# One pool of 2 KB slots, accumulators opened by ScalarE, and chunk products taken ahead of their norm, in a one-core encoder layer

## The chip, the core and the metric

The kernel runs on one core of a Trainium2 chip. TensorE (PE) does the matmuls, VectorE (DVE) and ScalarE (ACT) the elementwise work, SyncE (SP) issues nearly all DMAs. The metric is the device time of one execution in microseconds; the median of the runs shown counts.

## The reference, cut to what matters

One encoder layer over two token groups, a prompt of 1024 and a sample of 256 rows, width 1024, in float32:

```python
h = x + 0.5 * swiglu(rmsnorm(x, g1), w_gate1, w_up1, w_down1)      # d_ff = 2816
proj = rmsnorm(h, gm) @ w_in                                        # 22 units of 128 columns
a = rmsnorm(banded_sink_attention(rot(aq), rot(ak), av), ga)        # window 128, 8 heads, 2 kv heads
r = silu(rg) * normalise(retention_fwd + retention_bwd)             # 4 heads of 128, chunks of 128
h = h + concat([a, r]) @ w_out
h = h + 0.5 * swiglu(rmsnorm(h, g2), w_gate2, w_up2, w_down2)
y = rmsnorm(h, g_final)
# swiglu(x, wg, wu, wd) = (silu(x @ wg) * (x @ wu)) @ wd ;  rmsnorm(x) = x * rsqrt(mean(x^2)) * g
```

## The kernel before, in words

Everything is kept transposed: 1024 features on 8 tiles of 128 partitions (KT = 8), and the 1280 tokens along the free dimension in three chunks, c = 0 and c = 1 of 512 tokens (the prompt) and c = 2 of 256 (the sample). Each operand of a large matmul is split into a rounded high part and a low part (`split`: ACT casts "hi", DVE subtracts to get "lo"), and each product is three matmuls: hi·hi, hi·lo, lo·hi (`part`, line 452).

**The two feed-forward blocks** (`ffn`, line 564) have 22 blocks of 128 hidden columns, taken in pairs t and t+11, so 11 pairs. For each pair gate (m = 0) and up (m = 1) are computed, then the activations are split, stored to DRAM (`keep`) and read back later by the down projection. Pair 0 is computed directly (`direct`): for each of gate and up the chunks 2, 0, 1 in turn, two units each. Pairs 1 to 10 use a 7/8 scheme (`product`, `seven`, `combos`): the two 512-token chunks and the two halves of the width form 2x2 blocks, and seven products of sums and differences replace eight; chunk 2 is computed plainly beside them in the banks d1 and d2. Weights come as 128x256 tiles (`fetch(..., 256)`, 8 for each product), and the sums of weights are formed by DVE on 128x256 tiles. In the first block the first chunk computed (2) runs on x·g with the row factors of the norm multiplied in behind the product (`rows2`); chunks 0 and 1 are normed first (`first`, `second`, `normed`).

The down projection (`down`, line 686) runs over groups of pairs ([0], [1, 2], [3, 4], [5, 6], [7, 8]) and adds each PSUM result into the residual h by a DVE instruction (`add`). h, 24 tiles, is loaded by `h = load()` (line 733) before the first group; each group reads nine activation products for each pair back from DRAM (`act`). `down_last` does pairs 9 and 10 and closes with the next norm.

**The middle** projects the 22 units for each chunk (`project`), runs attention blocks and retention heads in between, and the output projection (`out_unit`).

**Memory.** Work tiles live in two rings of slots: class s2, 77 slots of 128x512 (2 KB a partition), and class s1, 66 slots of 128x256 (1 KB) (`NS2, NS1`, line 394). `big(W)` picks the class by width. PSUM has 8 banks.

**Order.** All operations are recorded in program order by `Weaver` and then ordered by a list scheduler (`order`, line 219): each engine takes, of the operations that are ready, the one recorded first; DMAs may run at most 300 operations ahead of the oldest matmul not yet placed; a slot must be free, and `may` keeps the order of slots safe. Durations come from a table (`cost`, line 141); a DMA issue is counted there as 0.05 us and 2.2 us to land. The result is a fixed order for each engine; at run time each instruction waits in its queue for its semaphores. All instructions are emitted from line 372, so the profile's rows are told apart by tile names: raw = a fetched weight, whi/wlo = its parts, xh/xl = parts of an activation or factor, xa = an activation read back, h = residual, pa/pb/pc = PSUM banks.

Of the kernel before, what the change touches and what calls it, by code (L numbers as in the profile page):

```python
# [12 lines left out]
P = 128  # L13
# [78 lines left out]
class Op:  # L92
    __slots__ = ("eng", "calls", "cost", "lat", "bufs", "deps", "idx", "wait", "succ", "ready", "allocs", "kind", "at")
# [6 lines left out]
class Weaver:  # L100
# [5 lines left out]
    AHEAD = 300  # L106
    ENG = {"tensor": "PE", "vector": "DVE", "scalar": "ACT", "gpsimd": "POOL", "sync": "SP"}
# [33 lines left out]
    def cost(eng, method, a, k, outs, ins):  # L141
        n = outs[0].box[3] - outs[0].box[2] if outs else 0
        if eng == "tensor":
            if method == "transpose":
                return 0.107
            r = ins[0].buf.args[2] == F32R
            if r:
                return n / 2400 + 0.0136

            side = outs[0].box[1] - outs[0].box[0] <= 64  # L150
            return max((2.2 if side else 4) * n / 2400, 0.11 if n == 1 else 0.213)
        m = max([n] + [v.box[3] - v.box[2] for v in ins])
        ps = any(v.buf.psum for v in ins)
        if eng == "scalar":
            if a[2:3] == (AF.Identity,):
                return 0.3
            return (0.05 if ps else 0.09) + m * 0.00084 + (0.19 if "accum_out" in k else 0)
# [4 lines left out]
        if method == "tensor_scalar":  # L162
            return 0.06 + n * 0.00104 + 0.06 * (len(ins) - 1)
        if method == "tensor_tensor_reduce":
# [7 lines left out]
    def record(self, calls):  # L172
# [3 lines left out]
        for eng, method, a, k in calls:  # L176
# [15 lines left out]
            for views, wr in ((ins, False), (outs, True)):  # L192
                for v in views:
# [15 lines left out]
                    if id(b) not in op.bufs:  # L209
                        op.bufs[id(b)] = b  # L210
                        b.left += 1
                        if b.order is None and b.tag is not None:
# [3 lines left out]
                            op.allocs.append(b)  # L216
        self.ops.append(op)

    def order(self):
        import heapq  # L220

        ops = self.ops

# [64 lines left out]
        while len(out) < len(ops):  # L288
            best = None
            for e in engs:  # L290
                lim = free[e] + SLACK
                while later[e] and later[e][0][0] <= lim:
                    heapq.heappush(now[e], heapq.heappop(later[e])[1])
                held = []
                pick = None
                while now[e]:
                    i = heapq.heappop(now[e])
                    if may(ops[i]):
                        pick = (max(free[e], ops[i].ready), i)
                        heapq.heappush(now[e], i)  # L300
                        break
                    held.append(i)
# [18 lines left out]
            if i in now[e]:  # L321
                now[e].remove(i)
# [62 lines left out]
def tile_encoder_layer(ctx: ExitStack, tc: tile.TileContext, xT, wf1, w_in, w_out, wf2,  # L385
# [8 lines left out]
    NS2, NS1 = 77, 66  # L394
# [11 lines left out]
    def s2(dt=F32, name="t"):  # L406
        return nc.tile(hp, [P, 512], dt, "s2", nm(name), NS2)

# [35 lines left out]
    def halves(t, W=512):  # L444
        hi, lo = big(W, F32R, "whi"), big(W, F32R, "wlo")
# [48 lines left out]
    def norm_split(h, gcol, W):  # L494
        pb = rms_rows(h, W)
        xh, xl = [], []
        for kt, x in enumerate(h):
# [3 lines left out]
            a = big(W, F32R, "xh")  # L501
            b = big(W, F32R, "xl")
# [5 lines left out]
    def normed(h, gcol, W):  # L508
        pb = rms_rows(h, W)
# [7 lines left out]

    def pair(t, W):
        a, b = big(W, F32R, "xh"), big(W, F32R, "xl")
# [13 lines left out]
    def seven(r11, r12, r21, r22):  # L533

        def tile1(name):
            return big(256, name=name)

        yield 1, halves(r11, 256)
        yield 2, halves(r12, 256)
        s1, s2_ = tile1("s1"), tile1("s2")  # L540
        nc.vector.tensor_tensor(s1, r21, r22, op=ALU.add)
        nc.vector.tensor_tensor(s2_, s1, r11, op=ALU.add)
        yield 6, halves(s2_, 256)
        s3 = tile1("s3")
        nc.vector.tensor_tensor(s3, r11, r21, op=ALU.add)
        yield 7, halves(s3, 256)
        yield 5, halves(s1, 256)
        yield 4, halves(r22, 256)
        yield 21, halves(r21, 256)
        s4 = tile1("s4")  # L550
        nc.vector.tensor_tensor(s4, s2_, r12, op=ALU.add)
        yield 3, halves(s4, 256)
# [11 lines left out]
    def ffn(tag, wsrc, xn, xp, x2, load, after, rows2=None):  # L564
# [4 lines left out]
        keep = {}  # L569

        def product(t, m):
# [6 lines left out]
            def both(ps, ws, x, W, start, stop):  # L578
                for k, w in enumerate(ws):
                    part(ps, w, x[2 * k:2 * k + 2], W, start and k == 0, stop and k == 1)  # L580

            for (i, w0), (_, w1) in zip(*(seven(*q) for q in r)):
                w = w0, w1
                if i == 1:
                    both(X, w, xs[1], 512, True, True)
                    both(d1, w, x2[:4], 256, True, False)
                    o11 = s2(name="o11")
                    nc.scalar.copy(o11, X)
                elif i == 2:
                    both(Z, w, xs[2], 512, True, True)  # L590
# [645 lines left out]
```

## Time and profile before

| | us |
|---|---|
| median of 3 runs | 2381.1 (2379.52 to 2383.1) |
| the profiled execution | 2384.64 |
| its span, first to last instruction | 2382.7 |
| PE busy in it | 2300.1 (97%) |
| DVE busy | 1664.0 (70%) |
| ACT busy | 1011.8 (42%) |

The span falls into the first feed-forward block (up to about 900 us), the middle (to about 1540 us) and the second block. The profile's views used here are: the page, the busy time of each engine in chosen stretches, the groups of instructions, the chain of work that ended last, the waits of one engine for another, and the instructions in order of time. All refer to this one execution.

### The profile page before, as it was taken

To read this page: it belongs to the slowest core of one execution; us is meant where nothing else is said; L and a number is where in the kernel's file an instruction comes from. 1 tells how busy PE (TensorE), PEld (TensorE's weight loads), DVE (VectorE), ACT (ScalarE), POOL (GpSimd) and SP (SyncE) were. 2 spreads that over 40 slices of the span, in tenths; PEclk is the share of its full clock that TensorE was granted. 3 is DMA by queue.
4 is the path that set the end of the run, shared out by engine and by line. 5 is a ranking of instruction groups with operands and counts; after the bars stand their busy time and mean duration, and the time that the engine had idled before them with its cause. 6 is when DMAs were issued, how large, how long until landed. Compare 5 with 4: busy or idle time off the path is not lost.

```text
span 2382.7 us, 35970 instructions
## 1 busy us (share of the span) xinstructions
PE 2300.1 (97%) x12354; PEld 1948.1 (82%) x12354; DVE 1664.0 (70%) x3639; ACT 1011.8 (42%) x2297; POOL 28.2 (1%) x31
## 2 busy tenths in 40 slices
PE   7999999999799999999999999999999999989998
PEld 6888888888688888886777878888888888868887
DVE  8677766675777866655677767956776766677866
ACT  6444444443222235235667555534444444322311
POOL 0000000000000000000000000000000000000000
PEclk8999999999899999999999999999999999999999
DMA  4233343338865443230115254223443335876622
GB/s 161 95 123 123 132 147 116 111 114 290 281 197 191 142 154 107 70 106 32 32 43 180 85 168 144 66 100 126 140 153 111 114 122 188 278 250 202 191 81 89
DMA packets 230296, 330.77 MB, mean 139 GB/s; under 512 B 25824, under 2 KB 113760, under 8 KB 230112
## 3 DMA queue, kind: packets, MB, share of 16 engines
q1 hardware_dynamic: 230112, 328.47, 41.2%
q8 instruction: 97, 1.59, 0.3%
q14 instruction: 87, 0.71, 0.1%
HBM read 226.65 MB, written 101.71 MB: 138 GB/s over the span
## 4 chain that ended last, share of the span: by engine, by line
PE 88%; DVE 3%; DMA 3%; ACT 3%; issue 1%; SPq 1%; POOL 0%; POOLq 0%; DVEq 0%; ACTq 0%
PE pa L372 61%; PE pb L372 26%; ACT prob L372 2%; DMA raw<-wf 1%; SPq L372 1%; DVE prob L372 1%; DVE xn L372 1%; DVE wlo L372 1%; ACT whi L372 0%; DVE o L372 0%; DMA xa<-a_7l 0%; PE pc L372 0%; DVE xl L372 0%; ACT pt L372 0%; DVE h L372 0%
## 5 line engine op out<-in xcount | busy, mean ns | idle before, releaser
L372 PE MATMUL pa<-xh,whi 128*128 128x512 f32 (+1 forms) x2576 | 921.6, 358 | 10.3 <-ACT whi L372 3.8
L372 PE MATMUL pa<-xh,wlo 128*128 128x512 f32 (+1 forms) x2576 | 911.8, 354 | 6.1 <-DVE wlo L372 6.0
L372 PE MATMUL pa<-xl,whi 128*128 128x512 f32 (+1 forms) x2576 | 912.1, 354 | 5.6 <-DVE xl L372 5.6
L372 PEld LDWEIGHTS pa<-xh,whi 128*128 128x128 f32 x2576 | 491.5, 191 | 86.7 <-ACT whi L372 8.6
L372 PEld LDWEIGHTS pa<-xh,wlo 128*128 128x128 f32 x2576 | 490.2, 190 | 78.9 <-DVE wlo L372 12.4
L372 PEld LDWEIGHTS pa<-xl,whi 128*128 128x128 f32 x2576 | 491.3, 191 | 69.4 <-DVE xl L372 6.5
L372 PE MATMUL pb<-xa,whi 128*128 128x512 f32 (+1 forms) x1968 | 526.3, 356 | 21.3 <-DVE h L372 18.6
L372 ACT CAST whi<-raw 128x256 fp32r<-128x256 f32 (+1 forms) x676 | 304.3, 473 | 444.1 <-PE pa L372 216.0
L372 PEld LDWEIGHTS pb<-xa,whi 128*128 128x128 f32 x1968 | 349.8, 191 | 77.2 <-DVE h L372 21.9
L372 DVE TENSOR_TENSOR wlo<-raw,whi 128x256 fp32r<-128x256 f32 (+1 forms) x676 | 327.6, 505 | 107.7 <-PE pa L372 53.3
L372 ACT CAST whi<-s 128x256 fp32r<-128x256 f32 x464 | 184.2, 406 | 412.6 <-DVE s L372 211.9
L372 PE MATMUL pb<-xa,wlo 128*128 128x512 f32 (+1 forms) x984 | 348.7, 354 | 3.2 <-DVE wlo L372 3.2
L372 DVE SCALAR_TENSOR_TENSOR h<-pb,h 128x512 f32<-128x512 f32 (+1 forms) x408 | 245.9, 623 | 61.8 <-PE pb L372 59.4
L372 DVE TENSOR_TENSOR wlo<-s,whi 128x256 fp32r<-128x256 f32 x464 | 191.5, 423 | 104.6 <-PE pa L372 53.2
L372 PEld LDWEIGHTS pb<-xa,wlo 128*128 128x128 f32 x984 | 187.5, 191 | 30.9 <-DVE wlo L372 4.4
L372 DVE TENSOR_TENSOR s<-raw,raw 128x256 f32<-128x256 f32 x232 | 97.9, 422 | 86.2 <-PE pa L372 78.7
L372 DVE TENSOR_TENSOR s<-s,raw 128x256 f32<-128x256 f32 x232 | 97.1, 423 | 52.0 <-PE pa L372 34.7
L372 DVE TENSOR_TENSOR o<-o,pa 128x512 f32<-128x512 f32 x120 | 82.2, 685 | 68.9 <-PE pa L372 36.4
L372 ACT ACTIVATE sq<-h 128x512 f32<-128x512 f32 (+1 forms) x96 | 50.4, 555 | 117.1 <-DVE h L372 101.1
L372 ACT CAST xh<-s 128x512 fp32r<-128x512 f32 (+1 forms) x114 | 60.3, 537 | 81.2 <-DVE s L372 56.9
L372 DVE TENSOR_TENSOR xl<-s,xh 128x512 fp32r<-128x512 f32 (+1 forms) x114 | 65.1, 585 | 19.5 <-ACT xh L372 12.7
L372 DVE TENSOR_TENSOR sq<-sq,sq 128x512 f32<-128x512 f32 (+1 forms) x93 | 55.7, 600 | 17.1 <-ACT sq L372 12.8
(126 smaller groups left out, 1644.0 us busy)
## 6 DMA issues: line engine op xcount, KB each, us to landing
raw<-wf SPq DMA_DIRECT2D x464, 128.0 KB, 2.5
raw<-w_in SPq DMA_DIRECT2D x132, 256.0 KB, 3.1
raw<-w_out SPq DMA_DIRECT2D x48, 256.0 KB, 3.1
raw<-wf SPq DMA_DIRECT2D x32, 256.0 KB, 3.6
h<-xT SPq DMA_DIRECT2D x32, 256.0 KB, 5.4
a_1h<-xh SPq DMA_DIRECT2D x22, 256.0 KB, 2.0
a_2h<-xh SPq DMA_DIRECT2D x22, 256.0 KB, 2.1
a_1l<-xl SPq DMA_DIRECT2D x22, 256.0 KB, 2.3
```

The source lines that it names most:

```text
L372: i = getattr(getattr(self.nc, eng), method)(*[r(x) for x in a], **{m: r(x) for m, x in k.items()})
```

## The change

- **Slots.** `NS2, NS1` become 104 and 12 (before 77 and 66; the same bytes). A split tile of at most 256 columns puts hi and lo beside each other in one 2 KB slot (`two`), also when it goes to DRAM and back (one DMA of 256 KB for what were two of 128 KB).
- **Weights.** `product` fetches 128x512 tiles (4 for each product), and `seven` works on width 512 there. `down` fetches its 256-column pieces in pairs with one DMA.
- **Residual.** `down` no longer loads h ahead: the first `add` to each of the 24 tiles is an ACT copy from PSUM with the scale in it. The residual of chunk 0, 1, 2 is loaded and added by DVE behind groups 1, 2, 3.
- **First reads of the down projection.** In the up product of the last pair, behind its second of eight pieces, the nine products of pair 0 are read back (`early`).
- **Pair 0.** `direct` now goes chunk by chunk with gate and up together. In the first block chunks 2 and 0 both run on x·g ahead of their norm; the row factors are multiplied in at gate and up. Chunk 1 is normed first, chunk 0 is normed afterwards for the later pairs. A chunk-2 product uses two PSUM banks for its four results.
- **Planner.** A DMA issue is counted as 0.47 us and 2.0 us to land; some other costs are corrected. The list scheduler runs four times; from each plan a due time of every operation is worked out, which gives DVE, ACT, POOL and SP a new priority for the next plan, and the plan with the shortest span by its own table is used.

```diff
-    NS2, NS1 = 77, 66
+    NS2, NS1 = 104, 12
+    def two(W, name):
+        if W <= 256:
+            t = s2(F32R, name)
+            return t[:, :W], t[:, 256:256 + W]
+        return s2(F32R, name + "h"), s2(F32R, name + "l")
...
-                op.cost, op.lat, op.kind = 0.05, 2.2, nb
+                op.cost, op.lat, op.kind = 0.47, 2.0, nb
...
     def order(self):
+        best, prio = None, list(range(len(self.ops)))
+        for _ in range(self.PASSES):
+            out = self.arrange(prio)
+            if best is None or self.span < best[0]:
+                best = self.span, out
+            due = self.due()
...
+                if op.eng == "PE" or due[op.idx] is None:
+                    prio.append(op.idx)
+                else:
+                    j = bisect.bisect(times, (due[op.idx], 1 << 60)) - 1
+                    prio.append(min(op.idx, times[max(j, 0)][1]))
...
-            r = [[fetch(wsrc[u, :, m, i * 512 + k * 256:i * 512 + k * 256 + 256], 256)
-                  for u in (t, t + HALF) for i in range(2)] for k in range(2)]
+            r = [fetch(wsrc[u, :, m, i * 512:i * 512 + 512]) for u in (t, t + HALF) for i in range(2)]
...
+    def raw_pair(x, kt, W):
+        g = par[:, G_F1 + kt:G_F1 + kt + 1]
+        a, b = two(W, "x")
+        nc.scalar.activation(a[:, :W], x[:, :W], AF.Copy, scale=g)
+        nc.vector.scalar_tensor_tensor(b[:, :W], x[:, :W], g, a[:, :W].bitcast(F32), op0=ALU.mult, op1=ALU.subtract)
+        return a, b
...
+        def up(s, x, W, rows):
+            nc.vector.tensor_tensor(s[:, :W], s[:, :W], x[:, :W], op=ALU.mult)
+            if rows is not None:
+                nc.vector.tensor_tensor(s[:, :W], s[:, :W], rows[:, :W], op=ALU.mult)
...
+            products(2)
+            products(0)
+            close(2)
+            lead.ready(1)
+            close(0)
+            products(1)
+            lead.ready(0)
+            close(1)
...
             def add(c, d, ps, sign):
                 W = CH[c][1]
-                nc.vector.scalar_tensor_tensor(h[c][d][:, :W], ps[:, :W], 0.5 * sign, h[c][d][:, :W],
-                                               op0=ALU.mult, op1=ALU.add)
+                if h[c][d] is None:
+                    h[c][d] = big(W, name="h")
+                    nc.scalar.activation(h[c][d][:, :W], ps[:, :W], AF.Copy, scale=0.5 * sign)
+                else:
+                    nc.vector.scalar_tensor_tensor(h[c][d][:, :W], ps[:, :W], 0.5 * sign, h[c][d][:, :W],
+                                                   op0=ALU.mult, op1=ALU.add)
...
+        def early(i):
+            if i == 2:
+                first.update({j: [act(0, j)] for j in (1, 2, 6, 7, 5, 4, 3, 8, 9)})
...
-        h = load()
-        for g in ([0], [1, 2], [3, 4], [5, 6], [7, 8]):
-            down(g, h)
+        groups = [[0], [1, 2], [3, 4], [5, 6], [7, 8]]
+        for n, g in enumerate(groups):
+            down(g, h, first if n == 0 else None)
+            if 1 <= n <= 3:
+                c = n - 1
+                W = CH[c][1]
+                for d in range(KT):
+                    t = load(c, d)
+                    nc.vector.tensor_tensor(h[c][d][:, :W], h[c][d][:, :W], t[:, :W], op=ALU.add)
```

## Rows read from the trace of the kernel before

**Rows 1.** The page: engine, busy us (share of the span), instructions.
```profile
PE 2300.1 (97%) x12354; PEld 1948.1 (82%) x12354; DVE 1664.0 (70%) x3639; ACT 1011.8 (42%) x2297; POOL 28.2 (1%) x31
```

**Rows 2.** Busy us (instructions) by stretch: PE, PEld, DVE, ACT, POOL; clock, DMA share, GB/s.
```profile
0.00:120.00 120.00, 105.03 (x531) 90.85 (x532) 89.93 (x172) 67.77 (x138) 3.93 (x7) 0.91 0.38 127
120.00:540.00 420.00, 415.99 (x2175) 351.89 (x2175) 289.21 (x639) 194.18 (x438) 0.00 (x0) 1.00 0.37 125
540.00:700.00 160.00, 145.31 (x732) 122.20 (x731) 110.36 (x247) 43.52 (x107) 0.00 (x0) 0.94 0.76 259
...
1100.00:1240.00 140.00, 127.86 (x796) 92.94 (x795) 91.57 (x277) 92.21 (x238) 4.31 (x4) 0.94 0.09 31
1240.00:1440.00 200.00, 190.02 (x1285) 162.42 (x1285) 147.48 (x405) 118.53 (x286) 9.70 (x10) 0.98 0.45 146
1560.00:2040.00 480.00, 480.00 (x2536) 414.25 (x2535) 319.18 (x671) 212.01 (x487) 0.00 (x0) 1.00 0.41 136
2040.00:2120.00 80.00, 69.41 (x349) 58.01 (x348) 54.42 (x120) 22.58 (x58) 0.00 (x0) 0.94 0.89 314
```

**Rows 3.** Groups by shape, PE, 1560 to 2040 us: busy us, mean ns, idle before.
```profile
L372 PE MATMUL pa<-xh,whi 128*128 128x512 f32 x545 | 213.1, 391 | 0.0
...
L372 PE MATMUL pa<-xh,whi 128*128 128x256 f32 x301 | 84.8, 282 | 0.0
```

**Rows 4.** The chain that ended last, projections of chunk 2: start us, us, what.
```profile
1312.01 16.19 PE pa L372 x135
```

**Rows 5.** Groups by shape, PE, 120 to 540 us.
```profile
L372 PE MATMUL pa<-xh,whi 128*128 128x512 f32 x460 | 182.3, 396 | 3.9 <-DVE o L372 3.4 <-ACT whi L372 0.5
...
L372 PE MATMUL pa<-xl,whi 128*128 128x256 f32 x265 | 75.0, 283 | 0.0
```

**Rows 6.** The chain that ended last, 0 to 60 us.
```profile
5.43 4.13 DMA raw<-wf
...
10.26 8.80 PE pa L372 x48
...
27.03 5.36 DVE xn L372 x8
```

**Rows 7.** DVE instructions in order of time, 48 to 60 us: start, us.
```profile
54.60 4.90 DVE L372 TENSOR_TENSOR xl<-xn,xh 128x512 fp32r<-128x512 f32 x8
```

**Rows 8.** DMA issues on SP's queue in order of time, 0 to 112 us.
```profile
1.17 3.74 SPq L372 DMA_DIRECT2D h<-xT  x8
```

**Rows 9.** The chain that ended last, 220 to 235 us.
```profile
228.36 4.25 DMA raw<-wf
```

**Rows 10.** Busy time by stretch again, three short stretches of the down projections.
```profile
720.00:780.00 60.00, 60.00 (x320) 51.70 (x319) 48.10 (x107) 16.08 (x41) 0.00 (x0) 1.00 0.54 175
...
600.00:620.00 20.00, 7.69 (x21) 5.20 (x21) 11.31 (x24) 4.42 (x11) 0.00 (x0) 0.58 0.97 321
2085.00:2095.00 10.00, 1.76 (x6) 1.15 (x5) 1.62 (x3) 0.00 (x0) 0.00 (x0) 0.66 0.94 300
```

**Rows 11.** The chain that ended last, whole span, at the first block's turn to down.
```profile
598.44 5.26 DMA xa<-a_4l
```

**Rows 12.** Waits, 2040 to 2120 us: who waited for whom, us, times, longest.
```profile
ACT whi L372 <- DMA a_9l<-xl: 16.8, 1, 16.8
...
PE pb L372 <- DVE h L372: 9.4, 3, 8.2
```

**Rows 13.** Groups by shape, whole span: accumulation by DVE, copy out of PSUM by ACT.
```profile
L372 DVE SCALAR_TENSOR_TENSOR h<-pb,h 128x512 f32<-128x512 f32 x312 | 211.6, 687 | 59.4 <-PE pb L372 57.5
...
L372 ACT COPY o<-pa 128x512 f32<-128x512 f32 x40 | 23.3, 582 | 25.5 <-PE pa L372 25.5
```

**Rows 14.** Waits on SP's queue, 1080 to 1320 us.
```profile
SPq L372 <- PE pb L372: 113.3, 19, 20.8
```

**Rows 15.** The page: DMA issues, count, KB each, median us to landing.
```profile
raw<-wf SPq DMA_DIRECT2D x464, 128.0 KB, 2.5
...
raw<-wf SPq DMA_DIRECT2D x32, 256.0 KB, 3.6
```

More of the change, by code (lines that the diff above doesn't have):

```diff
@@ L92 @@
 class Op:
-    __slots__ = ("eng", "calls", "cost", "lat", "bufs", "deps", "idx", "wait", "succ", "ready", "allocs", "kind", "at")
+    __slots__ = ("eng", "calls", "cost", "lat", "bufs", "deps", "idx", "wait", "succ", "ready", "allocs", "kind", "at", "first")
     def __init__(self, eng):
@@ L216, in record, with due, arrange @@
                             op.allocs.append(b)
+        op.first = list(op.allocs)
         self.ops.append(op)
     def order(self):
+        best, prio = None, list(range(len(self.ops)))
[4 more added lines that the diff above has]
+            due = self.due()
+            at = sorted((op.at, op.idx) for op in self.ops if op.eng == "PE")
+            times, k = [], 0
+            front = 0
+            for t, i in at:
+                front = max(front, i)
+                times.append((t, front))
+            import bisect
+            prio = []
+            for op in self.ops:
+                if op.eng == "PE" or due[op.idx] is None:
[3 more added lines that the diff above has]
+                    prio.append(min(op.idx, times[max(j, 0)][1]))
+        self.span, out = best
+        return out
+    def due(self):
+        due = [None] * len(self.ops)
+        for op in reversed(self.ops):
+            t = None
+            for i in op.succ:
+                s = self.ops[i]
+                x = s.at if s.eng == "PE" else due[i]
+                if x is not None and (t is None or x < t):
+                    t = x
+            if t is not None:
+                due[op.idx] = t - op.cost - op.lat
+        return due
+    def arrange(self, prio):
         import heapq
         ops = self.ops
+        for op in ops:
+            op.succ, op.ready, op.at = [], 0.0, None
+            op.allocs = list(op.first)
+            for b in op.bufs.values():
+                b.left = 0
+                b.end = 0.0
+        for op in ops:
+            for b in op.bufs.values():
+                b.left += 1
+        for t in self.tags.values():
+            t["free"] = [0.0] * t["cap"]
         for t in self.tags.values():
@@ L612, in product @@
+                hook(i)
             return [o11, X, o21, o22, d1, d2]
[L614 to L627 removed]
@@ L630, in gate_up, with seven_eighths @@
+        def seven_eighths(t, hook=lambda i: None):
+            r = last.rows(2)
             acts = []
-            for x in product(t, 0):
+            for x in product(t, 0, lambda i: None):
                 W = 512 if len(acts) < 4 else 256
-                s = big(W, name="s")
-                if W < 512 and rows2:
-                    nc.vector.tensor_tensor(s, x[:, :W], rows2[0], op=ALU.mult)
-                    x = s
-                nc.scalar.activation(s[:, :W], x[:, :W], AF.Silu)
-                acts.append(s)
```

277 lines of the change are left out of this document (165 added, 112 removed).

## The prediction

> **What bounds the kernel now.** The page comes first: PE is busy for 97% of the span [rows 1]. The change touches no large matmul's count or shape, so it can only win back time in which PE is idle, slowed by the clock, or held inside its busy time. The next view is busy time by stretch [rows 2]: 1560 to 2040 us, gate and up of the second block, has PE busy for 480.00 of 480 us. That stretch is the yardstick. The chunk-2 projections give 16.19/135 = 0.120 us for a 256-column matmul [rows 4]. With three kinds of matmul, the stretch holds 1635 matmuls of 512 columns and 901 of 256 [rows 3] (the other kinds count within one of these), so a 512-column one costs (480 - 901 x 0.120)/1635 = 0.2275 us.
>
> The losses against it, and the reader should look for each in its rows:
> - **Start, 0 to 120 us.** PE is idle for 15 us, and the clock is 0.91 [rows 2]. PE begins at 10.26 us, when the first weight has landed and been cast; it then stands through 27 to 33 us while DVE norms eight tiles [rows 6], and it stands again in the same way for the other chunk.
> - **Gate and up, first block, 120 to 540 us.** 3 x 460 x 0.2275 + 3 x 265 x 0.120 = 409.3 us of work in 420, so 10.7 are lost [rows 5], though PE shows only 4 idle [rows 2]. The chain names a weight landing late [rows 9]; such a stall stands in three of ten pairs.
> - **Turn from gate/up to down, first block.** 14.7 us idle in 540 to 700 [rows 2], most of it in 600 to 620, where PE works 7.7 of 20 us at clock 0.58 with the DMA engines at 0.97 [rows 10]. The chain there is transfers [rows 11]. Half of the busy time at the lower clock (1.2 GHz) adds about 4: 19 us lost.
> - **The same turn, second block.** 10.6 us idle [rows 2], 8.2 of them in 2085 to 2095 [rows 10], plus about 2 for the clock: 12.5 us. PE waits for h, DVE's accumulation, and ACT waits 16.8 us for a slot to come free by a store [rows 12].
> - **The middle, 1100 to 1440 us.** 12.1 + 10.0 us idle, clock 0.94 and 0.98 [rows 2]: 17 and 8 us at the lower level, which cost up to 10 more. SP waits 113 us for PE to free slots [rows 14] with DMA at 0.09 [rows 2]: weights that could fill the holes don't come in for want of slots.
>
> The page "Perfetto Trace Analysis" of the Trainium skill (Identifying the Most-Contended Engine) holds matmul busy time to be a poor measure and wants the weight loads' share. That share is 0.86 in the yardstick and 92.9/140 = 0.66 and 162.4/200 = 0.81 in the middle [rows 2], which by that rule puts about 44 us of headroom there instead of 22; with the same share won back as below, the sum would be some 4 us better.
>
> **The change part by part.** The sum is made against the profiled execution, 2384.6 us (span 2382.7 and 2 around it), which lies 3.5 above the median of 2381.1.
>
> *Start.* Chunk 2's first matmul needs four x tiles and one weight instead of eight and one: four issues at 3.74/8 = 0.47 us fewer [rows 8], about 2 us. Then 96 matmuls of 256 columns and 96 of 512 (11.5 and 21.8 us) run ahead of any norm, and chunk 1's norm is worked out under them, so the two stands go. But DVE gets more to do: eight low parts of chunk 0 by a two-operand instruction (5.36/8 = 0.67 us [rows 6], 5.4 us) and four products with rows (4.90/8 = 0.61 [rows 7], 2.4 us). I add up all that DVE must do before the fourth combination of pair 1 is ready: weights 4.8, chunk 2's low parts and squares 5.8, chunk 0's raw low parts 5.4, squares, norm and low parts of chunks 1 and 0 with row products and gating 36, 32 combinations and their low parts 19.6, pair 1's weights 6.8, small ones 1: 79 us. From 5.5 us on, at the share of 0.85 that DVE has early and nearly full later, it ends at about 89 us, when PE undisturbed would have wanted it at 83. So some 6 of the saved 15 come back: 8 us saved, between 3 and 12. What is late next is DVE, not the data.
>
> *Gate and up, first block.* Half as many weight DMAs, and a planner that counts an issue at 0.47 us, which the trace bears out [rows 8], where it had 0.05. The second block shows that this loop can run without loss [rows 2]. I take half of 10.7: 5 us, between -2 and 9. The second block has nothing to gain.
>
> *Turns.* The nine products of pair 0 (16 transfers, 4 MB) go into the slots of two dead factors some 17 us of PE work ahead of the end; 5 MB of h leave the queue; 24 of group 0's 36 accumulations (0.687 us on DVE) become ACT copies (0.582) [rows 13], which takes 14 us of DVE off a group whose matmuls last 25. A chunk-2 pair needs one slot. What stays: pair 10's stores, 3 MB, the group [1, 2] products, 8 MB, and weights still move at about 320 GB/s [rows 10] in the 45 us around the turn, about 16 MB, or 50 us. So the DMA queue stays the bound by a few us. 19 becomes 5 (14 saved, between 5 and 17) and 12.5 becomes 4.5 (8, between 3 and 11).
>
> *Down groups 1 to 3.* The residual loads, 24 transfers, lie on SP's queue behind the groups; each group lasts 50 us, and at a DMA share of 0.54 [rows 10] they are hidden. The 24 additions (8 x 0.69 + 8 x 0.69 + 8 x 0.42 = 14.3 us) fall on DVE, which is at 48.1 of 60 [rows 10], so 40 of a group's 50 us becomes 45.6. PE never stops there now; with 5 banks to a column block and 8 in all a late DVE is felt at once. -3 us for both blocks, between 0 and -8.
>
> *Middle.* 27 more large slots, eight of them taken by chunk 2's factors, and due times for the elementwise work. With the holes' cause in the slots [rows 14], I take 0.4 of the 32 us: 13, between -10 and 30, since no row shows the new order. The 12 small slots, eight of which hold chunk 2's residual, force the sample's four retention heads one behind another; 87 us of output projection (384 matmuls of 0.2275) stand beside them, which hides it. The tail and the merged stores cost nothing: PE is busy beside the stores.
>
> Sum: 8 + 5 + 14 + 8 - 3 + 13 = 45. 2384.6 - 45 = 2339.6, and 3.5 less to stand with the median: **2336**.
>
> **The rivals.**
> - *DVE and the DMA queue take it back* (2371). The start stays on DVE, the turns on transfers, and the new plan of the middle gives little: 3 + 2 + 5 + 3 - 8 + 5 = 10. For it: DMA at 0.97 over 20 us at the turn [rows 10]. Against: h's 5 MB and 14 us of DVE really leave it. That the early reads are planned late, because slots aren't free, ends here or between here and the forecast.
> - *The middle fills up* (2303). 12 + 8 + 17 + 11 + 0 + 30 = 78. For it: 113 us of waiting for slots [rows 14]. Against: a long chain of scores, exponentials and transposes that slots don't shorten.
> - *Slower: weights late in every product* (2396). A 256 KB weight lands in 3.6 us where 128 KB took 2.5 [rows 15], the wider cast adds 0.2 us and the wider low part 0.27: about 1.5 us later for the first piece. The weights now share 40 slots, beside 64 held by factors, with activations waiting for their stores. If they can't be asked for a product ahead, each of 40 products stands 1.5 us: 60 us, less the 45. It decides from 45/40 = 1.1 us a product on. For it: the late weight at 228 us [rows 9]. Against: 480 us without one idle us under nearly the same bytes of slots [rows 2].
> - *No change* (2381): the middle's new order loses some 30 us and eats the rest. Nothing in the trace speaks for it but that the order is new.
>
> The same page of the Trainium skill (DMA Optimizations) says that splitting DMAs lets some work start sooner where the DMA engines are mostly idle; here, at a share of 0.41 [rows 2], loads are merged. That rule speaks for the slower rival; by it the time would be its 2396, and the stretch without a stall speaks against its weight here.
>
> **How the numbers follow.** Forecast 0.60 (its own range 2318 to 2358), taken back 0.17, middle fills 0.10, slower 0.08, no change 0.05. About 0.2%, 4.8 us, is what a measurement of this kernel can tell from no change. Faster: 0.60 + 0.17 + 0.10 = 0.87; same 0.05; slower 0.08. The range takes in the two rivals on the faster side: 2303 to 2376.
>
> **What would show it.** Right: PE starts before 8.5 us and has no hole over 3 us up to 60 us; the turns' stretches idle under 5 us each; DVE near 46 of 50 us in groups 1 and 2 with PE full; SP's waits for PE in the middle well under 113 us. Wrong: idle PE in 70 to 100 us waiting for low parts of combinations by more than 10 us (start), DMA at 1.0 with idle PE at the turns (queue), ACT casts waiting for raw weights in most pairs (slower rival), more idle PE in 1100 to 1440 than 22 us (middle).

## The result and the profile after

The kernel after takes 2320.0 us (median of 4 runs, 2318.28 to 2321.1) against 2381.0 for the kernel before: a ratio of 0.9742 (95% interval 0.9726 to 0.9759), 61 us. The forecast of 2336 was 16 us too slow; its direction and its range held. The profiled execution took 2319.39 us with a span of 2317.5.

The page of the kernel after, busy time by engine, answers to [rows 1]:

```profile
PE 2270.6 (98%) x12354; PEld 1937.2 (84%) x12354; DVE 1589.7 (69%) x3171; ACT 970.6 (42%) x2034; POOL 26.8 (1%) x31
```

As many matmuls as before, 29.5 us less of PE's busy time and 35.7 us less of idle time. The busy time in stretches of [rows 2] and [rows 10], kernel after (columns as in [rows 2]):

```profile
0.00:120.00 120.00, 112.96 (x574) 96.30 (x575) 103.17 (x181) 75.00 (x135) 3.19 (x7) 0.96 0.42 146
120.00:540.00 420.00, 412.04 (x2175) 354.73 (x2174) 262.89 (x439) 161.28 (x296) 0.00 (x0) 1.00 0.36 127
720.00:780.00 60.00, 59.91 (x314) 50.77 (x313) 49.83 (x112) 14.97 (x39) 0.00 (x0) 1.00 0.73 253
1100.00:1240.00 140.00, 139.95 (x977) 111.84 (x976) 112.98 (x354) 108.43 (x281) 6.56 (x7) 1.00 0.24 80
1240.00:1440.00 200.00, 199.64 (x1302) 176.26 (x1301) 153.31 (x355) 110.73 (x248) 10.54 (x11) 1.00 0.41 138
1560.00:2040.00 480.00, 472.46 (x2490) 406.25 (x2490) 293.41 (x506) 196.22 (x381) 0.00 (x0) 1.00 0.43 150
```

The turns from gate/up to down come earlier in the kernel after, so they are compared by the 20 us behind the last gate/up matmul. First block, before and after:

```profile
597.80:617.80 20.00, 7.99 (x28) 5.47 (x26) 9.32 (x20) 3.18 (x7) 0.00 (x0) 0.64 0.99 338
587.10:607.10 20.00, 17.63 (x93) 14.77 (x92) 11.46 (x27) 11.53 (x26) 0.00 (x0) 1.00 1.04 384
```

What to see: the middle, 1100 to 1440, has 0.4 us of idle PE where it had 22.1. At the first turn PE stands for 2.4 of 20 us at the full clock, where it stood for 12; at the second, behind 2018.8, for 1.1, where it stood for 7.4. Gate and up of the first block, 120 to 540, hold 2175 matmuls, exactly as many as before: nothing was won there. And the yardstick of the prediction, 1560 to 2040, which had no idle time at all, now has 7.5 us of it, 6.5 of them before gate and up end at 2018.8.

**How the stages are told apart here.** All stages but one pair end at a point that the trace names: the last matmul on a gate/up bank or the first on a read-back activation (tile xa). Between the two down projections lie the middle and the second gate/up, which overlap. They are parted by the last 552 us ahead of the second down projection. In the kernel before this stretch is nearly all gate and up:

```profile
900.40:1520.90 620.50, 598.37 (x3463) 492.02 (x3462) 423.70 (x1014) 331.04 (x744) 19.96 (x20) 0.98 0.30 97
1520.90:1572.90 52.00, 46.34 (x243) 40.26 (x242) 40.66 (x83) 20.11 (x46) 0.50 (x1) 0.93 0.12 42
1520.90:2072.90 552.00, 545.59 (x2888) 471.22 (x2887) 375.26 (x792) 243.59 (x561) 0.50 (x1) 0.99 0.41 136
```

Matmuls of 512 and of 256 columns cost differently, so what this stretch got done is counted by shape (groups by shape, PE, 1520.9 to 2072.9 us; the other kinds of matmul come in the same numbers):

```profile
L372 PE MATMUL pa<-xh,whi 128*128 128x512 f32 x609 | 238.3, 391 | 0.8 <-ACT o L372 0.8
...
L372 PE MATMUL pa<-xh,whi 128*128 128x256 f32 x352 | 100.0, 284 | 0.0
```

With three kinds, that is 1828 matmuls of 512 columns (one of the down projection among them) and 1056 of 256; 4 small ones are left out. At the prediction's prices, 0.2275 and 0.120 us, this is 542.6 us of work. A kernel that gets less of it done in its last 552 us has lost the difference there, and has done the rest earlier. The kernel after, the same stretches (the middle, the first 52 us of the second gate/up, and all of its 552), and its groups by shape in 1466.8 to 2018.8 us:

```profile
874.60:1466.80 592.20, 591.36 (x3543) 496.44 (x3542) 421.96 (x1022) 324.81 (x743) 19.78 (x20) 1.00 0.30 100
1466.80:1518.80 52.00, 44.01 (x208) 36.85 (x207) 28.27 (x48) 21.18 (x38) 0.00 (x0) 0.93 0.35 122
1466.80:2018.80 552.00, 536.71 (x2808) 461.32 (x2807) 326.13 (x549) 215.48 (x408) 0.00 (x0) 0.99 0.38 133
```

```profile
L433 PE MATMUL pa<-xh,wh 128*128 128x512 f32 x606 | 238.5, 394 | 7.3 <-DVE o L433 7.3
...
L433 PE MATMUL pa<-x,wh 128*128 128x256 f32 x660 | 121.7, 282 | 0.0
L433 PE MATMUL pa<-x,wl 128*128 128x256 f32 x330 | 93.3, 283 | 0.0
```

That is 3 x 606 = 1818 of 512 columns and 660 + 330 = 990 of 256, 532.4 us of work, so the second gate/up lost 10.2 us. The two stages together went from 1172.5 to 1144.2 us, so the middle gained 28.3 + 10.2 = 38.5. The same working for every kernel run, each change against the kernel before, in us. The stages are read from one execution of each kernel, which lies up to 4.4 us from the median; the medians of the last column are from 4 runs each, and each ratio is to the kernel before run beside them (2381.0 to 2382.7):

| kernel | gate/up 1, with the start | down 1 | middle | gate/up 2 | down 2 | median, ratio (interval) |
|---|---|---|---|---|---|---|
| after | -10.7 | -15.1 | -38.5 | +10.2 | -10.7 | 2320.0, 0.9742 (0.9726 to 0.9759) |
| old_plan | -1.2 | -14.1 | -23.4 | +26.5 | -9.3 | 2359.0, 0.9904 (0.9890 to 0.9919) |
| new_plan | -14.1 | -14.9 | +2.2 | -8.6 | -7.8 | 2340.8, 0.9822 (0.9806 to 0.9839) |
| one_pass | -2.9 | -16.8 | -38.4 | +19.3 | -10.6 | 2335.5, 0.9804 (0.9790 to 0.9819) |
| cheap_dma | -7.4 | -14.6 | -37.9 | +17.2 | -8.0 | 2333.5, 0.9788 (0.9773 to 0.9803) |
| new_plan1 | -10.0 | -13.1 | +4.1 | +0.2 | -11.5 | 2354.4, 0.9879 (0.9864 to 0.9893) |
| slots100 | +2.9 | -14.7 | -36.8 | +43.6 | -12.1 | 2366.4, 0.9930 (0.9915 to 0.9944) |
| rings80 | -6.3 | -19.1 | -20.9 | +0.5 | -12.5 | 2325.2, 0.9754 (0.9740 to 0.9769) |
| no_turn | -8.1 | -17.8 | -38.3 | +16.3 | -12.1 | 2324.5, 0.9756 (0.9741 to 0.9770) |
| norm_first | -6.3 | -16.1 | -38.5 | +11.8 | -11.6 | 2323.7, 0.9754 (0.9738 to 0.9771) |
| direct2 | -14.5 | -13.1 | -38.2 | +19.1 | -11.7 | 2326.9, 0.9767 (0.9752 to 0.9781) |
| narrow | -1.2 | -16.5 | -38.8 | -1.1 | -10.5 | 2316.8, 0.9726 (0.9711 to 0.9740) |
| mixed2 | -12.4 | -12.4 | -39.1 | -2.7 | -10.9 | 2308.4, 0.9688 (0.9672 to 0.9705) |

In direct2, 5.5 of the second gate/up's us are 24 more matmuls, which its edit adds there. All eight kernels that have the 104 slots of after and at least a part of its planner's changes gain the same 38 to 39 us in the middle.

So two things happened that the prediction did not have: the middle gave three times its term, and the second gate/up, "nothing to gain", lost 10 us. One caution for all that follows: every kernel is planned anew, so an edit also moves stages that it does not touch. no_turn differs from after by 6 us in the second gate/up, where nothing of its edit lies; a difference of that size in one stage of one run is not evidence.

### The profile page after: what moved, and what is told of

Read it like the earlier page. It is cut to its first block, busy times and chain, and to the rows that moved or that the text cites. A ratio compares the mean times of both kernels' runs of the same rounds, so it can differ in the third digit from the quotient of the medians.

```text
span 2317.5 us, 34127 instructions
## 1 busy us (share of the span) xinstructions
PE 2270.6 (98%) x12354; PEld 1937.2 (84%) x12354; DVE 1589.7 (69%) x3171; ACT 970.6 (42%) x2034; POOL 26.8 (1%) x31
## 4 chain that ended last, share of the span: by engine, by line
PE 89%; DVE 5%; DMA 4%; issue 1%; ACT 1%; SPq 0%; POOL 0%; POOLq 0%; DVEq 0%; ACTq 0%
PE pa L433 63%; PE pb L433 25%; PE pc L433 2%; DMA raw<-wf 1%; DMA xa<-a 1%; DVE s L433 1%; DVE wl L433 1%; DVE h L433 1%; DMA h<-xT 1%; DVE o L433 1%; DVE xl L433 0%; DVE w L433 0%; DMA raw<-w_in 0%; DVE t L433 0%; SPq L433 0%
## 5 line engine op out<-in xcount | busy, mean ns | idle before, releaser
L433 PE MATMUL pa<-xh,wh 128*128 128x512 f32 x1664 | 659.9, 397 | 19.3 <-DVE o L433 15.3
L433 PE MATMUL pa<-xh,wl 128*128 128x512 f32 x1664 | 649.8, 390 | 8.0 <-DVE wl L433 8.0
L433 PE MATMUL pa<-xl,wh 128*128 128x512 f32 x1664 | 651.4, 391 | 1.0 <-DVE xl L433 1.0
L433 PE MATMUL pb<-xa,w 128*128 128x512 f32 (+1 forms) x2376 | 453.5, 352 | 6.0 <-ACT h L433 3.4
L433 PEld LDWEIGHTS pb<-xa,w 128*128 128x128 f32 x2376 | 386.4, 189 | 73.2 <-DVE h L433 6.3
L433 PEld LDWEIGHTS pa<-xh,wh 128*128 128x128 f32 x1664 | 314.0, 189 | 87.2 <-DVE o L433 19.1
L433 PEld LDWEIGHTS pa<-xh,wl 128*128 128x128 f32 x1664 | 313.5, 188 | 75.7 <-DVE wl L433 8.4
L433 PEld LDWEIGHTS pa<-xl,wh 128*128 128x128 f32 x1664 | 314.2, 189 | 58.7 <-DVE xl L433 1.8
L433 PE MATMUL pa<-x,wh 128*128 128x256 f32 x1824 | 337.5, 284 | 0.0
L433 PEld LDWEIGHTS pa<-x,wh 128*128 128x128 f32 x1824 | 294.9, 191 | 12.3
```

The source lines that it names most:

```text
L433: i = getattr(getattr(self.nc, eng), method)(*[r(x) for x in a], **{m: r(x) for m, x in k.items()})
```

## The experiments

The theory from the prediction: slots win the middle, fewer bytes and less DVE work win the turns. The rival: the new planner (costs and due times) makes most of the gain, and the memory and work edits little.

### Memory and planner apart

old_plan is the kernel after with the planner of the kernel before (its cost table, its single pass, operations taken in recorded order); new_plan is the kernel before with the planner of the kernel after. The core of both edits (old_plan takes these lines out, new_plan puts them in):

```diff
-                op.cost, op.lat, op.kind = 0.05, 2.2, nb
+                op.cost, op.lat, op.kind = 0.47, 2.0, nb
...
+        for _ in range(self.PASSES):
+            out = self.arrange(prio)
...
-                    heapq.heappush(now[e], heapq.heappop(later[e])[1])
+                    i = heapq.heappop(later[e])[1]
+                    heapq.heappush(now[e], (prio[i], i))
```

> The changed kernel with the planner of before (one plan, priority by program order, 0.05 us for a DMA issue). Theory 'slots': the middle is full because the one large ring has spare slots for weights; most of the 61 us stays, the time is 2328 to 2342 and idle PE in the middle (875 to 1440 us) stays under 8 us. Rival 'plan': the due times fill the middle; then some 30 us come back, 2348 to 2360, with 20 us or more of idle PE there.

> The kernel before with only the new planner (four plans, due times, 0.47 us for a DMA issue), its slots and work unchanged. 'Plan': it takes 30 us or more off, 2340 to 2352, with the middle nearly free of holes. 'Slots': at most 15 us off, 2366 to 2378, the holes of 1100 to 1440 us stay at 15 us or more, and the turns stay.

Measured: 2359.0 and 2340.8. Against the kernel before run beside them, the planner alone gives some 42 us, the other edits alone some 23, both 61. By the totals the planner is the larger part and the parts nearly add. Both times lie in the range of 'plan'. The stages say otherwise. Middle and second gate/up, first old_plan, then new_plan:

```profile
885.10:1508.70 623.60, 612.61 (x3628) 509.12 (x3627) 433.08 (x1040) 332.05 (x758) 20.30 (x20) 1.00 0.29 97
1508.70:2060.70 552.00, 525.90 (x2722) 449.62 (x2721) 310.14 (x510) 204.58 (x381) 0.00 (x0) 0.98 0.38 130
```

```profile
871.40:1485.50 614.10, 588.84 (x3422) 487.67 (x3421) 413.04 (x993) 321.38 (x723) 19.21 (x19) 0.97 0.30 97
1485.50:2037.50 552.00, 552.00 (x2930) 477.02 (x2929) 381.17 (x813) 253.48 (x580) 0.98 (x1) 1.00 0.40 135
```

The planner alone wins nothing in the middle (+2.2; PE idle for 25 us there, against 22 before) and all that it wins outside it: both turns, a second gate/up without an idle us, and a first one that is as full (kernel new_plan):

```profile
120.00:540.00 420.00, 420.00 (x2225) 362.58 (x2224) 295.42 (x644) 196.58 (x446) 0.00 (x0) 1.00 0.40 136
```

The memory and work edits alone win 23 us in the middle and give 27 back in the second gate/up. The turns are won by either (-14.1 and -14.9 in the first block, -15.1 with both). Neither theory holds for the whole; each holds for its stage. That the totals nearly add is an accident of these terms: the turns don't add (either side has nearly all of it) and the middle does more than add.

### What in the planner

one_pass has the kernel after plan once, so without due times; cheap_dma has it count a DMA issue as before; new_plan1 is new_plan with one pass.

```diff
-    PASSES = 4
+    PASSES = 1
```

```diff
-                op.cost, op.lat, op.kind = 0.47, 2.0, nb
+                op.cost, op.lat, op.kind = 0.05, 2.2, nb
```

> The changed kernel with its own costs but one plan only, priority by program order: due times taken out. 'Plan': most of the middle's 36 us come back, 2345 to 2355. 'Slots': 2325 to 2338, the middle stays nearly full and what is lost is spread over the turns and the start.

> The changed kernel whose planner counts a DMA issue as 0.05 us and 2.2 us to land again, all else as changed. If the truer issue cost is what the corrected table is worth (old_plan to one_pass, 23 us), 12 us or more come back, 2332 to 2345, with gate and up waiting for weights. If the other corrected costs and the due times carry it, 2317 to 2326.

> The kernel before with the new planner's costs but one plan, without due times. In the changed memory the due times were worth 15 us (one_pass). If they are worth the same here, 2352 to 2360; if the two full turns and the full gate and up of new_plan come from the costs, 2340 to 2348, and the down stretches stay under 291 us.

Measured: 2335.5 (as 'slots' had it), 2333.5 and 2354.4 (each in the first of its two ranges). Beside the memory of after, due times are worth 15.5 us and the issue cost 13.5; beside that of before, the new costs are worth some 28 us and due times another 13.6. In the kernel after neither touches the middle (-38 in both runs); most of what they are worth lies in the two gate/up stages, where one_pass and cheap_dma lose 9 and 7 us in the second block and 8 and 3 in the first. Beside the old memory the new costs with a single plan already win both turns (new_plan1: -13.1 and -11.5), so the turns need no due times. That a plan which prices an issue at 0.05 us, where the queue needs 0.47 [rows 8], asks for weights too late is the likely reading; the waits don't settle it. What lifts the middle from old_plan's -23 to -38 is neither of the two by itself; whether it is both together or the other corrected costs was not run.

### The slots

slots100 takes four slots from the kernel after; rings80 gives new_plan's two rings three large slots more for six small ones.

```diff
-    NS2, NS1 = 104, 12
+    NS2, NS1 = 100, 12
```

```diff
-    NS2, NS1 = 77, 66
+    NS2, NS1 = 80, 60
```

> The changed kernel with 100 large slots instead of 104, all else the same, planned anew. 'Slots': the ring is near the point where weights come late in every product (the slower rival's mechanism); four slots less cost 20 us or more, 2340 or above, with ACT casts waiting for raw weights. 'Plan': the planner works around four slots; 2318 to 2328.

> new_plan (the kernel before with the new planner) with six small slots of 1 KB made into three large ones (80 and 60 instead of 77 and 66). 'Slots': the two stages pull against each other; the middle's idle PE falls from 25 us to 20 or less, and gate and up, which ran full, begins to wait for weights (5 us idle or more in 500), so the time is 2343 to 2365. Rival: three slots tell nothing; 2337 to 2343 and both stages as in new_plan.

slots100: 2366.4, 46 us slower than after, for 4 slots in 104. PE's waits in 1570 to 2010:

```profile
PE pa L433 <- DVE wl L433: 21.9, 6, 6.0
```

The middle stays won (-36.8). What is lost is gate and up: 33 us more than in after in the second block and 14 in the first, and in both PE waits for the low parts of weights (wl). The weights themselves are not late: ACT, which casts them, waits for a weight's transfer for 1.3 us in 1516 to 2068, so the sign that was expected, casts waiting for raw weights, is missing. The chain that ended last shows what is, at three of the six waits in the same way; one of them:

```profile
1843.18 0.63 ACT xh L433
...
1843.83 2.07 DMA a<-xh
...
1846.02 0.69 DVE wl L433
```

An activation is split and stored, and the low part of a weight comes right behind the end of that store, which fits a slot that the activation holds until then. So the shortage that the prediction named for its slower rival, weights beside "activations waiting for their stores", is there four slots away from the kernel after, at a price of 46 us; but it does not strike in every product, and not by transfers asked for too late.

rings80: 2325.2, 15.6 us faster than new_plan, below what either reading had expected. Its two stretches:

```profile
875.00:1475.10 600.10, 587.59 (x3469) 490.89 (x3469) 416.05 (x1003) 324.08 (x737) 19.84 (x20) 0.99 0.31 100
1475.10:2027.10 552.00, 545.71 (x2882) 470.05 (x2881) 367.68 (x790) 246.04 (x560) 0.00 (x0) 0.99 0.39 133
```

Three large slots turn new_plan's middle from +2.2 to -20.9, and idle PE there falls from 25 to 12.5 us. That the middle wants large slots is thereby shown for 23 of its 38.5 us, with nothing but the rings (and so the plan) changed. It pays with 8 us at the start and first gate/up and 9 in the second, and gains 9 in the two down stages. With the planner, a better split of the old rings is within 5 us of the whole change.

SP's wait for PE to free slots in 1080 to 1320, the row on which the prediction built [rows 14]: first the kernel after, then rings80; new_plan has 88.0 us:

```profile
SPq L433 <- PE pb L433: 108.7, 21, 22.1
```

```profile
SPq L433 <- PE pb L433: 28.6, 15, 6.1
```

With PE full in this stretch the kernel after waits 108.7 us, as before; new_plan waits less and its middle is not better; rings80 waits a quarter and its middle is only half won. The prediction's sign, waits "well under 113 us", failed where the middle did fill up. This sum doesn't measure a want of slots: a queue that runs ahead waits for whatever comes free last.

### The turns

no_turn is the kernel after with the residual loaded ahead, all accumulations by DVE, and no early reads of the first group.

```diff
-            finish(t, seven_eighths(t, *[early] * (t == HALF - 1)))
+            finish(t, seven_eighths(t))
...
-            h[c] = [None] * KT
+            h[c] = [load(c, d) for d in range(KT)]
...
-            down(g, h, first if n == 0 else None)
-            if 1 <= n <= 3:
-                c = n - 1
-                W = CH[c][1]
-                for d in range(KT):
-                    t = load(c, d)
-                    nc.vector.tensor_tensor(h[c][d][:, :W], h[c][d][:, :W], t[:, :W], op=ALU.add)
+            down(g, h)
```

> The changed kernel with both edits to the turn undone: h is loaded ahead of the groups and every accumulation is DVE's, and the first reads are not put into the last product. If these edits win the turns (the prediction's theory), 15 to 22 us come back: 2335 to 2342, with down at some 298 us from the first to the last read-back matmul in each block. If the planner or the slots win them, which new_plan hints at (287.7 and 290.0 us for the down stretches without the edits), the time is 2317 to 2326 and these stretches stay under 291 us.

Measured: 2324.5, 4.5 us slower than after, and not at the turns. The first down projection is even 2.7 us shorter than that of after (284.8 against 287.5), and the second one 1.4 (285.7 against 287.1). The first 20 us behind the last gate/up matmul in no_turn:

```profile
589.70:609.70 20.00, 20.00 (x108) 17.21 (x107) 19.55 (x36) 1.03 (x2) 0.00 (x0) 1.00 1.05 394
```

PE is full with the DMA engines' share read as 1.05, at 394 GB/s; new_plan has 19.12 of 20 us (583.70 to 603.70) at a share of 1.04. So the three edits that were made at the turn, and on which the prediction's 22 us rested above all, aren't needed for it beside the new planner, and the new planner cures it beside the old memory. Beside the old planner it is open: old_plan has its turns cured too, but holds these three edits together with the memory, and no run takes them out there. no_turn's loss lies in the gate/up stages: 6.1 in the second, 2.6 in the first.

### The start

norm_first norms chunk 0 ahead of pair 0, as before the change (chunk 2 still runs ahead of its norm). direct2 computes pairs 0 and 1 directly in both blocks, so that the combinations aren't needed until pair 2.

```diff
         def x(self, c, k):
-            if c != 1:
+            if c == 0 and c not in self.n:
+                self.n[0] = normed(load_x(0), G_F1, 512)
+                self.pairs[0] = [pair(t, 512) for t in self.n[0]]
+            if c == 2:
...
-            if c == 1:
+            if c != 2:
                 return None
...
-            x = load_x(1) if c == 1 else self.raw[0]
-            self.n[c] = normed(x, G_F1, 512, self.r[0] if c == 0 else None)
+            if c == 0:
+                return
+            self.n[c] = normed(load_x(1), G_F1, 512)
```

```diff
-    ffn(1, wf1, lead1(), lambda a: factors((a.n[0], a.n[1]), (a.pairs[0], a.pairs[1])), load1, after1, 1)
+    ffn(1, wf1, lead1(), lambda a: factors((a.n[0], a.n[1]), (a.pairs[0], a.pairs[1])), load1, after1, 2)
...
-    ffn(2, wf2, leads2(), lambda a: factors(nx, xp), load2, after2, 1)
+    ffn(2, wf2, leads2(), lambda a: factors(nx, xp), load2, after2, 2)
```

> The changed kernel with chunk 0 of the first block normed ahead of its products, as before; gate and up of a chunk stay together. If computing chunk 0 ahead of its norm is worth what the start gained, 5 to 9 us come back: 2325 to 2329, with a hole of some 8 us between 25 and 45 us. If DVE's combinations are the bound of the first 110 us anyway, the hole only moves: 2318 to 2323, and the wait for combinations at 90 to 105 us shrinks by as much as the new hole takes.

> The changed kernel with pairs 0 and 1 of both blocks computed directly. This adds 2 x 24 matmuls of 512 columns, 11 us in all, and gives DVE one more pair of PE work to make the combinations under. If the waits for combinations (some 8 us with the lower clock at 94 to 105 us, 8 us at 1503 to 1515 us) vanish fully, the time is 2313 to 2318; if only a part goes, 2320 to 2328.

norm_first: 2323.7, 3.7 slower, between the two ranges. Its stretches 15 to 60 and 60 to 120, and behind them those of after:

```profile
15.00:60.00 45.00, 37.33 (x178) 31.42 (x178) 37.30 (x67) 28.17 (x51) 3.60 (x3) 0.89 0.40 145
60.00:120.00 60.00, 58.32 (x292) 49.07 (x292) 49.18 (x81) 31.49 (x56) 0.00 (x0) 1.00 0.31 108
```

```profile
15.00:60.00 45.00, 44.20 (x254) 39.07 (x253) 39.40 (x71) 30.19 (x57) 2.99 (x3) 0.96 0.34 126
60.00:120.00 60.00, 54.95 (x230) 43.75 (x230) 54.86 (x91) 34.03 (x58) 0.00 (x0) 0.94 0.37 132
```

Ahead of its norm PE gains 6.9 us up to 60 us and gives 3.4 back behind, where DVE, at 54.86 of 60, is late. direct2 removes that hole (-14.5 against -10.7 up to the first down projection), but computes eight products where seven would do, 5.5 us of work in each block. The second gate/up, where PE still stands for 8.6 us in the first 52, takes 8.9 us more than in after, and the middle is the same: 2326.9.

### The second gate/up

narrow forms sums and low parts of weights on 256-column halves, with the weights still loaded 512 wide. mixed2 does this in the second block alone (tag 2), and has pairs 0 and 1 direct in the first block alone, by the first of direct2's two edits.

```diff
+            def part(ps, ws, x, W, start, stop):
+                for k, w in enumerate(ws):
+                    whole(ps, w, x[2 * k:2 * k + 2], W, start and k == 0, stop and k == 1)
...
-            for i, w in seven(*r, 512):
+            for (i, w0), (_, w1) in zip(*(seven(*[x[:, k * 256:k * 256 + 256] for x in r], 256) for k in range(2))):
+                w = w0, w1
```

> The changed kernel, but the weights of the gate and up products are split and summed on 256 columns again (the DMAs stay 256 KB wide). Theory 'grain': the 512-wide weight operations stand ahead of the accumulation that PE waits for, 0.8 us in each pair and more in slots100; with narrow ones the second block's gate and up runs full as in new_plan (PE idle under 2 us of 500, 7 before) and the first block's 120 to 587 us too: 10 to 15 us less, 2304 to 2312. Rival 'slots': the stalls come from too few slots for weights, whatever the width; 2317 to 2325, the same idle PE.

> The changed kernel with pair 1 of the first block computed directly as well, and the weight operations of the second block's gate and up on 256 columns. direct2 took 3.8 us off the first block's gate and up, narrow 11.6 us off the middle and the second block's; if the two are independent, 2303 to 2309. If each came from its plan as a whole and not from its stage, 2313 to 2322.

Where the kernel after stands, from PE's waits, 1480 to 2018 us:

```profile
PE pa L433 <- DVE wl L433: 8.0, 1, 8.0
PE pa L433 <- DVE o L433: 7.3, 9, 0.8
```

and the chain that ended last in after, at the hole between pair 0 and pair 1, and at one of the nine short waits:

```profile
1511.11 2.49 DVE xl L433 x4
1513.61 0.61 DVE wl L433
```

```profile
1680.49 1.29 DVE wl L433 x2
1681.79 0.60 DVE s L433
1682.39 0.60 DVE wl L433
1682.99 0.61 DVE o L433
```

The hole: DVE forms low parts of combinations (xl) one behind another and gets to the weight's low part last. The short wait: the accumulation `o` stands behind four 512-wide operations on weights, and the bank that it would free is wanted. The first pair's stretch and the 500 us behind it in narrow, then the first 120 us of mixed2 and its first pair's stretch:

```profile
1463.30:1515.30 52.00, 52.00 (x284) 45.30 (x283) 31.68 (x66) 19.75 (x40) 0.56 (x1) 1.00 0.20 70
1515.30:2015.30 500.00, 494.68 (x2611) 425.80 (x2610) 324.70 (x744) 216.24 (x539) 0.00 (x0) 1.00 0.41 140
```

```profile
0.00:120.00 120.00, 118.23 (x625) 103.31 (x626) 94.72 (x169) 68.98 (x127) 2.89 (x7) 0.99 0.43 150
1454.30:1506.30 52.00, 52.00 (x284) 45.28 (x283) 31.89 (x67) 18.55 (x38) 1.04 (x1) 1.00 0.20 71
```

narrow: 2316.8, 3.2 below after, which is not clear of the scatter (2315.7 to 2319.8 against 2318.3 to 2321.1), and between the two ranges. But its second gate/up is back at the level of before (-1.1), and the hole is gone. The width alone does not make that hole: before, with 256-wide operations, has 5.7 us idle in its first 52 us of the stage, with DVE's combinations ahead of the weight's low part in the same way (its chain):

```profile
1536.02 2.50 DVE xl L372 x4
...
1544.01 0.70 DVE wlo L372
```

rings80 and new_plan1 have 5.3 and 5.7 there; new_plan, also with 256-wide ones, has none. What holds throughout is the whole stage: it loses 10 to 44 us in all eight kernels with 512-wide weight operations in it, and lies between -8.6 and +0.5 in the five with 256-wide ones. So the width costs this stage some 11 us (narrow against after); how much of the hole is the order's stays open. The waits for `o` fall only to 5.2 us in 6, and in the first block they stay (8.4 us in 7 between 120 and 596, 8.0 in 8 in after), so the width is not their whole cause; rings80, with two rings and 256-wide weights, has 0.9 us of them there. What else makes them stays open. The first block loses 9.5 us with narrow, its 536 matmuls in the first 120 us against 574: DVE, the engine that is short there, has more instructions (207 against 181). mixed2 keeps wide operations in the first block and lets a second direct pair cover the combinations there: 2308.4, 12 us below after and 74 below the kernel before run beside it, and the fastest version.

## Why the prediction was right, and where not

By its own terms, in us won, predicted and then measured. The terms add up to 45 and 65:

- **Start: 8, measured 9.** 574 matmuls instead of 531 in 0 to 120 us: 34 more of 512 columns and 9 more of 256, 8.8 us at the prediction's prices. PE begins with the first weight at 6.98 us instead of 10.26 and runs on without the stand of [rows 6], and DVE is late for pair 1 as worked out, at about 92 to 101 us. Kernel after:

```profile
90.00:95.00 5.00, 3.18 (x18) 2.23 (x16) 4.97 (x9) 3.51 (x7) 0.00 (x0) 1.00 0.23 82
95.00:100.00 5.00, 2.13 (x6) 1.15 (x6) 4.96 (x9) 2.53 (x5) 0.00 (x0) 0.81 0.00 0
100.00:105.00 5.00, 4.64 (x12) 3.54 (x12) 5.00 (x10) 3.49 (x7) 0.00 (x0) 0.51 0.00 0
```

  PE idles 5.1 us of these 15 with DVE at 14.9, and after it idled for 4.7 of the first ten us it works 4.6 of the last five at a granted 0.51, the lower level of its clock, 1.2 GHz. But the mechanism carries less than its size suggests: norm_first shows some 4 us for running ahead of the norm, no more than a new order alone can move.
- **Gate and up, first block: 5, measured 0 to 2.** The 120 to 540 stretch has its 2175 matmuls as before; the remaining 1.9 of the stage's 10.7 lie behind it. Of the reasons given, the planner's true issue cost does not show by itself (cheap_dma has the same work in this stretch as after), but the planner as a whole does: new_plan fills it without a gap (2225 matmuls). The change's other edits give it back, in after to waits for `o`; which of them does is open, since narrow has these waits too.
- **Turns with the down groups: 14 + 8 - 3 = 19, measured 25.8** (15.1 and 10.7). The size was near; the cause is not the one that was priced, at least beside the new planner: no_turn keeps the turns without the three edits. Order is enough to cure the loss of [rows 10]: new_plan does it with the old transfers, and new_plan1 with the new costs and a single plan. PE is full there at a DMA share of 1.05, so the transfers that the chain named [rows 11] were no bound. What in the order cures it, and which of the other edits cure it in old_plan, stays open; the priced ones may. DVE in 720 to 780 is at 49.83 of 60 with PE full; the feared tight spot didn't come.
- **Middle: 13, measured 38.5.** The step that failed is the factor 0.4 on 32 us, taken "since no row shows the new order". The cause, slots, was right as far as rings80 goes, 23 us, though the row that it was read from says nothing. The upper bound of 30 was too low as well: idle PE in the whole stage fell by 21.3 us (22.1 to 0.8), and 17 more were won inside PE's busy time, of which the slow clock was taken at 10 at most. The page "Perfetto Trace Analysis" of the Trainium skill (Identifying the Most-Contended Engine), which wants the weight loads' share rather than matmul busy time, put 44 us of headroom here. The trace agrees that there was more than idle time: that share rose from 0.66 and 0.81 to 111.84/140 = 0.80 and 176.26/200 = 0.88, though these stretches hold other work now, and 38.5 us came out of the whole stage.
- **Gate and up, second block: 0, measured -10.** The prediction read a stretch without idle time as one in which nothing moves. It has something to lose: DVE operations twice as wide hold up what stands behind them. And there was something to gain: the yardstick starts at 1560 and leaves out the hole behind pair 0, and new_plan wins 8.6 us in the stage. The slower rival, with 1.5 us for each of 40 products, was the nearest to the loss; the 20 products of the second block cost 10 us, a third as much each. The weights themselves land later than was taken (kernel after, the page's DMA issues: 4.3 us against 2.5 and the estimate of 3.6 [rows 15]):

```profile
raw<-wf SPq DMA_DIRECT2D x264, 256.0 KB, 4.3
```

  but PE's waits name no weight transfer, in the kernel after or in slots100; what is late in slots100 is the weight's low part, by its chain for want of a slot.

So the two large errors, +25.5 in the middle and -10 in the second gate/up, point opposite ways, and the rest was near in size. That the total came within 16 us is luck in part, and so is the turns' size, which was reached without the cause that was priced. The rival "the middle fills up" was the true one in its place; its 2303 would have needed the second gate/up to stay whole, and mixed2, where it does, comes to 2308.

## What to carry to other kernels

A change of memory and a change of order should be run apart and compared by stage, not by total: here the totals nearly add up while no stage does. A stretch with PE at 100% is not safe; ask of every operation made wider what stands behind it on its engine, and of every pool how many slots it is away from standing still. The sum of a queue's waits for free slots says nothing on whether slots are short; a run with three slots more or four fewer does.

## What the hardware showed that was not expected

DVE's instructions overlap at their ends. Kernel after, DVE in order of time at the short wait shown above (start, us, instruction):

```profile
1681.70 0.69 DVE L433 TENSOR_TENSOR s<-s,raw 128x512 f32<-128x512 f32 x1
1682.31 0.68 DVE L433 TENSOR_TENSOR wl<-raw,wh 128x512 fp32r<-128x512 f32 x1
1682.91 0.68 DVE L433 TENSOR_TENSOR o<-o,pa 128x512 f32<-128x512 f32 x1
```

They start 0.60 to 0.61 us apart and last 0.68 to 0.69 each, so sums of DVE work at 0.69 us, as in the prediction's 8 x 0.69, are about an eighth too large where DVE runs without a gap. "Perfetto Trace Analysis" of the Trainium skill (Optimizing Scalar/DVE Operations) gives each DVE instruction an access overhead of about 60 ns on SBUF, and says that the profiled latency holds about twice that, since the half for the write acknowledgement overlaps with the next instruction. The trace agrees that they overlap, by 0.08 us.
